# Depthwise convolution of two layers: seven taps off TensorE, eight onto ScalarE with GpSimd, the rest on VectorE

## Chip, cores and metric

The program runs on one core of one Trainium2 chip. The metric is the time of one execution on the device in microseconds; the value before is the median of three runs, 2263.01 us (2261.5 to 2263.6). A profiled execution gives the trace that is read below.

## What is computed

A network of two blocks with two layers each runs over 256 tokens of width 1024 in float32. The change lies in the mixing step of the second block, which occurs twice (once per layer). There, a depthwise convolution of 31 taps runs over 512 channels, and its result goes through a layer norm and a gate into the output product:

```python
CONV_DIM = 512
CONV_WIDTH_2 = 31

c_val, c_gate = jnp.split(c, 2, axis=-1)
c = c_val * jax.nn.sigmoid(c_gate)
c = depthwise_conv(c, conv_w[i], conv_b[i])     # y[s, ch] = b[ch] + sum_j w[j, ch] * c[s + j - 15, ch]
c = jax.nn.silu(layer_norm_2(c, conv_ln_g[i], conv_ln_b[i]))
y_conv = c @ w_conv_out[i]
...
h = h + (g_attn * y_attn + g_conv * y_conv) @ w_o[i]
```

## The kernel before

Activations lie with 128 channels on the partitions and the 256 tokens along the free dimension, so a channel's tap is a column of 128 factors and a shifted window of 256 tokens. Every large product is done in three passes with split operands: `wload` (L133) loads a weight tile of 128x1024 on the SP queue, ScalarE rounds it to `hi` (L145), VectorE takes the remainder as `lo` (L146), and `mm3` (L182) multiplies on TensorE at L184, L185 and L186. In this stage there are six buffers for `hi` and six for `lo` (four in one pool, two in another), so ScalarE can round a tile only when TensorE has finished with the one six tiles earlier.

The mixing step of the second block is `mix_b` (L1118). It multiplies in this order: three pairs of query, key and value columns, then four pairs for the convolution (L1224 to L1228), then eight gate pairs (L1230 to L1235); a pair is 128 output rows twice, two weight tiles and 48 matmuls. After each pair the planner `Order` (L310) is moved on by a fixed cost, and it then emits the small steps of generators that are due: the four steps of attention, two heads each (`attention_b`), and four convolution chunks (`conv`, L1202) of 128 channels each. A number that a generator yields is its own estimate of how long the step lasts. After the last gate pair, `O.finish` (L1267) emits what is left of attention and convolution. Then come the layer norm of the convolution (`norm`, L1240), the product of the attention's result (L1269) beside it, and the product of the convolution's result (L1276). The scheduler of the tile framework sets the final order on each engine's queue; each engine runs its queue in that order.

One chunk of `conv` makes the padded input `cp` (L1208). Its first seven taps (`PTAPS`) are matmuls: ScalarE writes a diagonal matrix `dg` of the tap's factors (L1214) and TensorE multiplies it with a shifted window of `cp` into a PSUM bank `rec` (L1215). ScalarE then moves the sum with the bias to `cy` in SBUF (L1218), and VectorE adds the other 24 taps one by one in place (L1220). The four `cy` are summed on TensorE against a matrix of ones for the mean (L1243), VectorE subtracts it (L1246), and so on through a reciprocal at L1256.

Of the kernel before, what the change touches and what calls it, by code (L numbers as in the profile page):

```python
# [8 lines left out]
F32 = mybir.dt.float32  # L9
F32R = mybir.dt.float32r  # L10
AF = mybir.ActivationFunctionType
# [4 lines left out]
MUL, ADD, SUB, MAX = ALU.mult, ALU.add, ALU.subtract, ALU.max  # L16

S = 256
# [4 lines left out]
C1 = -0.5 * math.exp(-0.5)  # L23
ADA_EVERY = 0.67
ADA_BUFS = 2
PTAPS = 7
ADA_PE = 2
FILL = {("f", 0): ((0, 0), (0, 1)), ("f", 1): ((1, 0), (1, 1))}
PBANKS = (4, 2, 2)
# [1088 lines left out]
def mix_b(G, L, x, l, mp, bias, dbg=None):  # L1118
    nc = G.nc
    mm = nc.tensor.matmul  # L1120
    tt = nc.vector.tensor_tensor
    stt = nc.vector.scalar_tensor_tensor
    act = nc.scalar.activation
    ident = G.c("ident", 128)
# [5 lines left out]
    cwh = L.pool.tile([128, 124], F32, tag="cwh", name=G.nm("cwh"))  # L1130
# [68 lines left out]
    cy = [None] * 4  # L1199
    pmu = []  # L1200

    def conv(i, t):  # L1202
        act(t[:, S:], t[:, S:], AF.Tanh, scale=0.5)
        cp = mp.tile([128, S + 30], F32, tag="cp", name=G.nm("cp"), bufs=3)
        nc.vector.memset(cp[:, 0:15], 0.0)
        nc.vector.memset(cp[:, S + 15:], 0.0)
        yield 0.5
        stt(cp[:, 15:S + 15], t[:, S:], 1.0, t[:, :S], ADD, MUL)  # L1208
        dg = []
        yield 1.0  # L1210
        ps = G.rec()
        for jj in range(PTAPS):
            d = mp.tile([128, 128], F32, tag="dg", name=G.nm("dg"), bufs=4)
            act(d, ident, AF.Copy, scale=cwh[:, jj * 4 + i:jj * 4 + i + 1])  # L1214
            mm(ps[:, :S], d, cp[:, jj:jj + S], start=jj == 0, stop=jj == PTAPS - 1)  # L1215
        yield 0.5 * PTAPS
        y = mp.tile([128, S], F32, tag="cy", name=G.nm("cy"), bufs=4)
        act(y, ps[:, :S], AF.Identity, bias=L.col("cb", i))  # L1218
        for jj in range(PTAPS, 31):
            stt(y, cp[:, jj:jj + S], cwh[:, jj * 4 + i:jj * 4 + i + 1], y, MUL, ADD)  # L1220
            yield 0.6
        cy[i] = y

    for i in range(4):  # L1224
        t = mp.tile([128, 512], F32, tag="cvg", name=G.nm("t"), bufs=1)
        tt(v3(t, 2), v3(pair(3 + i), 2), rb, MUL)
        O.add(f"c{i}", conv(i, t), 0.6)
        O.advance(cost)  # L1228
# [55 lines left out]
    for dp in range(4):  # L1284
        w = G.wload(G.ins["w_o"][l, dp], 2048)
        for i in range(2):
            ps = G.ps()
# [320 lines left out]
```

## Time and profile before

| | before |
|---|---|
| median of 3 runs | 2263.01 us |
| profiled execution, its own time | 2264.67 us |
| span from its first to its last instruction | 2262.9 us |
| TensorE busy | 2204.6 us, 97% |
| VectorE busy | 1681.6 us, 74% |
| ScalarE busy | 1276.6 us, 56% |
| GpSimd busy | 12.7 us |
| mean granted TensorE clock | 0.991 |

The profiled execution lasts 1.8 us longer than its span and 1.7 us longer than the median. A busy TensorE means that some matmul is under way, since their records overlap; it does not mean that matmuls follow each other as fast as they can. Shares over the whole span hide the stage of the change: this stage is about 105 us long in each of two layers (from 1328 us and from 1899 us after the span's start), and it is there that the trace has to be read.

### The profile page before, as it was taken

The numbers are of one execution on the slowest core, as the hardware profiler recorded it, in microseconds if no ns is written. First come the engines' busy times: TensorE is split into PE (matmuls) and PEld (weight loads), VectorE is DVE, ScalarE is ACT, GpSimd is POOL, SyncE is SP. The second block draws the span as 40 slices with busy tenths as digits, with TensorE's granted clock in tenths as the row PEclk, the third lists the DMA queues.
The fourth block names the chain that finished last, engine by engine and source line by source line (L and its number), as shares of the span: only waits on it lengthen the run. The fifth ranks groups of instructions, "written<-read, shape, count | busy, mean of one in ns | idle before, by whom it ended". The sixth has DMA issues, their size and how long they took to land.

```text
span 2262.9 us, 46464 instructions
## 1 busy us (share of the span) xinstructions
PE 2204.6 (97%) x18878; PEld 2134.0 (94%) x18878; DVE 1681.6 (74%) x3041; ACT 1276.6 (56%) x2160; POOL 12.7 (1%) x26
## 2 busy tenths in 40 slices
PE   4999999999999999999999999999999999999999
PEld 4989999999888899999999999999999999999999
DVE  5787878877678878876576569976577656997665
ACT  3575645654567645655454567654465446765444
POOL 0000000000000000000100000000000000000000
PEclk9999999999999999999999999999999999999999
DMA  7644457867554356755775652655566565256553
GB/s 281 195 146 145 139 192 263 271 220 260 187 167 145 121 168 227 264 185 157 177 231 159 199 170 88 203 182 177 164 199 196 165 189 177 94 179 198 182 162 120
DMA packets 127522, 415.35 MB, mean 184 GB/s; under 512 B 15019, under 2 KB 17707, under 8 KB 127308
## 3 DMA queue, kind: packets, MB, share of 16 engines
q1 hardware_dynamic: 124668, 407.23, 57.2%
q0 software_dynamic: 768, 2.10, 0.6%
q8 instruction: 148, 2.42, 0.4%
q10 hardware_dynamic: 1872, 3.06, 0.4%
q14 instruction: 66, 0.54, 0.1%
HBM read 408.92 MB, written 3.41 MB: 182 GB/s over the span
## 4 chain that ended last, share of the span: by engine, by line
PE 61%; DVE 2%; ACT 1%; DMA 1%; issue 0%; SPq 0%; ACTq 0%; DVEq 0%
PE ps L184 19%; PE ps L185 19%; PE ps L186 19%; PE aux L158 1%; PE rec L1215 1%; DMA raw<-in_ffn_in 1%; DVE lo L146 1%; ACT hi L145 0%; PE aux L1104 0%; DMA raw<-in_w_out 0%; PE aux L268 0%; DMA raw<-in_ffn_up 0%; DVE cy L1220 0%; ACT dg L1214 0%; PE aux L282 0%
## 5 line engine op out<-in xcount | busy, mean ns | idle before, releaser
L184 PE MATMUL ps<-h,hi 128*128 128x256 f32 x5088 | 1439.1, 284 | 13.7 <-ACT h L221 8.8
L186 PE MATMUL ps<-h,lo 128*128 128x256 f32 x5088 | 1434.0, 282 | 1.2 <-DVE lo L146 1.2
L185 PE MATMUL ps<-l,hi 128*128 128x256 f32 x4032 | 1136.8, 283 | 4.1 <-DVE l L222 3.9
L145 ACT CAST hi<-raw 128x1024 fp32r<-128x1024 f32 (+1 forms) x724 | 704.4, 976 | 629.2 <-PE ps L185 406.4
L146 DVE TENSOR_TENSOR lo<-raw,hi 128x1024 fp32r<-128x1024 f32 (+1 forms) x724 | 819.5, 1134 | 318.8 <-ACT hi L145 316.5
L184 PEld LDWEIGHTS ps<-h,hi 128*128 128x128 f32 x5088 | 961.5, 189 | 25.2 <-ACT h L221 10.2
L186 PEld LDWEIGHTS ps<-h,lo 128*128 128x128 f32 x5088 | 962.0, 189 | 5.3 <-issue 2.2
L185 PEld LDWEIGHTS ps<-l,hi 128*128 128x128 f32 x4032 | 763.4, 189 | 10.2 <-DVE l L222 4.8
L185 PE MATMUL ps<-h,hi 128*128 128x256 f32 x1056 | 298.9, 283 | 0.0
L185 PEld LDWEIGHTS ps<-h,hi 128*128 128x128 f32 x1056 | 198.6, 188 | 1.9 <-issue 0.5
L221 ACT CAST h<-t 128x256 fp32r<-128x256 f32 x148 | 59.6, 405 | 135.4 <-DVE t L1034 93.6
L222 DVE TENSOR_TENSOR l<-t,h 128x256 fp32r<-128x256 f32 x148 | 62.6, 424 | 50.1 <-ACT h L221 50.0
L362 DVE SCALAR_TENSOR_TENSOR ada<-ada,cact 128x1024 f32<-128x1024 f32 x80 | 96.6, 1215 | 2.1 <-DMA ada<-in_w_ada 2.1
L1031 DVE TENSOR_TENSOR t<-ps,r 128x512 f32<-128x512 f32 x88 | 60.7, 690 | 39.3 <-PE ps L186 39.0
L1220 DVE SCALAR_TENSOR_TENSOR cy<-cp,cwh,cy 128x256 f32<-128x256 f32 x192 | 85.1, 477 | 3.2 <-ACT cy L1218 2.9
L235 ACT ACTIVATE t<-x 128x256 f32<-128x256 f32 x96 | 37.6, 406 | 16.8 <-DVE x L1002 7.7
L1034 DVE TENSOR_TENSOR t<-t,t 128x256 f32<-128x256 f32 x88 | 36.8, 419 | 7.2 <-ACT t L1033 7.2
L1033 ACT ACTIVATE t<-t 128x256 f32<-128x256 f32 x88 | 36.2, 412 | 8.5 <-DVE t L1031 7.6
L210 PE MATMUL ps<-hi,h 128*128 128x256 f32 x128 | 37.7, 294 | 0.0
L242 DVE TENSOR_TENSOR t<-t,t 128x256 f32<-128x256 f32 x87 | 36.5, 419 | 1.6 <-ACT t L237 0.3
L212 PE MATMUL ps<-lo,h 128*128 128x256 f32 x128 | 37.4, 293 | 0.0
L248 PE MATMUL aux<-ones,t 128*128 128x1 f32 x68 | 11.0, 267 | 20.9 <-DVE t L242 17.5
(325 smaller groups left out, 1959.8 us busy)
## 6 DMA issues: line engine op xcount, KB each, us to landing
raw<-in_w_in SPq DMA_DIRECT2D x176, 512.0 KB, 4.4
raw<-in_ffn_in SPq DMA_DIRECT2D x176, 512.0 KB, 4.5
raw<-in_ffn_up SPq DMA_DIRECT2D x88, 512.0 KB, 4.6
ada<-in_w_ada SPq DMA_DIRECT2D x80, 512.0 KB, 5.0
raw<-in_ffn_out SPq DMA_DIRECT2D x64, 384.0 KB, 3.1
raw<-in_ffn_out SPq DMA_DIRECT2D x64, 320.0 KB, 3.1
raw<-in_w_branch SPq DMA_DIRECT2D x24, 512.0 KB, 3.8
raw<-in_ffn_down SPq DMA_DIRECT2D x32, 384.0 KB, 3.5
```

What stands on the lines that cost most here:

```text
L145: nc.scalar.copy(hi[:, :m], raw[:, :m])
L146: nc.vector.tensor_tensor(lo[:, :m], raw[:, :m], hi[:, :m], SUB)
L184: mm(ps, w[0], x[0], start=first, stop=False)
L185: mm(ps, w[0], x[1], start=False, stop=False)
L186: mm(ps, w[1], x[0], start=False, stop=last)
L210: mm(ps[:, :256], x[k][0][:, sl], h, start=k == 0, stop=False)
L221: nc.scalar.copy(h, src)
L222: nc.vector.tensor_tensor(l, src, h, SUB)
L235: nc.scalar.square(sq, x[k])
L362: nc.vector.scalar_tensor_tensor(raw, raw, 1.0, cact, MUL, MUL, accum_out=mods[f // 8][:, f % 8:f % 8 + 1]))
L1031: nc.vector.tensor_tensor(v3(gu, 2), v3(ps, 2), rb, MUL)
L1220: stt(y, cp[:, jj:jj + S], cwh[:, jj * 4 + i:jj * 4 + i + 1], y, MUL, ADD)
```

## The change

The matmul taps and their diagonal matrices are gone, and the accumulators lie in SBUF. Of a chunk's 31 taps, tap 0 goes to ScalarE together with the bias, taps 1 to 22 stay on VectorE, and the last eight (`GTAPS`) are multiplied on ScalarE: the first into a second accumulator `cyg`, each of the other seven into one buffer `cyt`, from which GpSimd adds it to `cyg`. At the end VectorE adds `cyg` to `cy`. Chunks 2 and 3 begin their taps only when chunk 0 and chunk 1 are done.

```diff
-PTAPS = 7
+GTAPS = 8
...
-        dg = []
+        def wt(jj):
+            return cwh[:, jj * 4 + i:jj * 4 + i + 1]
+
+        def other(jj):
+            if jj == 31 - GTAPS:
+                act(yg, cp[:, jj:jj + S], AF.Copy, scale=wt(jj))
+            else:
+                u = mp.tile([128, S], F32, tag="cyt", name=G.nm("cyt"), bufs=1)
+                act(u, cp[:, jj:jj + S], AF.Copy, scale=wt(jj))
+                nc.gpsimd.tensor_tensor(yg, yg, u, ADD)
         yield 1.0
-        ps = G.rec()
-        for jj in range(PTAPS):
-            d = mp.tile([128, 128], F32, tag="dg", name=G.nm("dg"), bufs=4)
-            act(d, ident, AF.Copy, scale=cwh[:, jj * 4 + i:jj * 4 + i + 1])
-            mm(ps[:, :S], d, cp[:, jj:jj + S], start=jj == 0, stop=jj == PTAPS - 1)
-        yield 0.5 * PTAPS
+        while i >= 2 and cy[i - 2] is None:
+            yield 0.5
         y = mp.tile([128, S], F32, tag="cy", name=G.nm("cy"), bufs=4)
-        act(y, ps[:, :S], AF.Identity, bias=L.col("cb", i))
-        for jj in range(PTAPS, 31):
-            stt(y, cp[:, jj:jj + S], cwh[:, jj * 4 + i:jj * 4 + i + 1], y, MUL, ADD)
+        acc, yg = y, mp.tile([128, S], F32, tag="cyg", name=G.nm("cyg"), bufs=2)
+        act(acc, cp[:, 0:S], AF.Identity, scale=wt(0), bias=L.col("cb", i))
+        rest = list(range(31 - GTAPS, 31))
+        for jj in range(1, 31 - GTAPS):
+            if rest and jj % 2:
+                other(rest.pop(0))
+            stt(acc, cp[:, jj:jj + S], wt(jj), acc, MUL, ADD)
             yield 0.6
+        tt(y, acc, yg, ADD)
         cy[i] = y
```

In VectorE's queue, the end of the first layer's convolution stood like this before; the first row is the last of the eight gate pairs, L1220 are taps, L146 are the remainders of weight tiles, L1246 begins the norm:

```order
L1232 TENSOR_TENSOR gate_17837<-ps_17850,r_16494 128x512
L1220 SCALAR_TENSOR_TENSOR cy_17266<-cp_17063,cwh_16496,cy_17266 128x256
L146 TENSOR_TENSOR lo_17973<-raw_17970,hi_17972 128x1024
L1220 SCALAR_TENSOR_TENSOR cy_17266<-cp_17063,cwh_16496,cy_17266 128x256
L146 TENSOR_TENSOR lo_18055<-raw_18052,hi_18054 128x1024
L1220 SCALAR_TENSOR_TENSOR cy_17266<-cp_17063,cwh_16496,cy_17266 128x256
L146 TENSOR_TENSOR lo_18061<-raw_18058,hi_18060 128x1024
L222 TENSOR_TENSOR l_17951<-aux_17934,h_17950 128x256
L1246 SCALAR_TENSOR_TENSOR cy_16968<-rec_18002,cy_16968 128x256
```

The same place of VectorE's queue now (taps are L1229, the addition of the second accumulator is L1231, the norm begins at L1256); between the last gate pair and the first row here stand 15 taps and one L222:

```order
L222 TENSOR_TENSOR l_17931<-aux_17920,h_17930 128x256
L1229 SCALAR_TENSOR_TENSOR cy_17655<-cp_17018,cwh_16496,cy_17655 128x256
L1231 TENSOR_TENSOR cy_17533<-cy_17533,cyg_17534 128x256
L1229 SCALAR_TENSOR_TENSOR cy_17655<-cp_17018,cwh_16496,cy_17655 128x256
L146 TENSOR_TENSOR lo_17967<-raw_17964,hi_17966 128x1024
L1229 SCALAR_TENSOR_TENSOR cy_17655<-cp_17018,cwh_16496,cy_17655 128x256
L146 TENSOR_TENSOR lo_17973<-raw_17970,hi_17972 128x1024
L1229 SCALAR_TENSOR_TENSOR cy_17655<-cp_17018,cwh_16496,cy_17655 128x256
L146 TENSOR_TENSOR lo_18055<-raw_18052,hi_18054 128x1024
L1231 TENSOR_TENSOR cy_17655<-cy_17655,cyg_17656 128x256
L1283 SCALAR_TENSOR_TENSOR gate_17048<-gate_17048,ps_17976 128x512
```

Between the last gate pair and the norm there were three taps; now there are 19 and two additions.

In ScalarE's queue, in the middle of the first layer's convolution, rows stood like this before, with the semaphores that each waits for (L145 rounds a weight tile, L1214 makes diagonal matrices):

```order
L145 CAST hi_17198<-raw_17196 128x1024 [waits DMAHW1_49,PE_49]
L145 CAST hi_17204<-raw_17202 128x1024 [waits DMAHW2_49,PE_49]
L1203 ACTIVATE t_16876<-t_16876 128x256 [waits DVE_49,Activation_49]
L1214 ACTIVATE dg_16955<-ca,cwh_16496 128x128 [waits PE_49]
L1214 ACTIVATE dg_16958<-ca,cwh_16496 128x128 [waits PE_49]
L1214 ACTIVATE dg_16961<-ca,cwh_16496 128x128 [waits PE_49]
```

The same queue now (L1217 is a tap's product for GpSimd, L1224 starts an accumulator):

```order
L1217 ACTIVATE cyt_17033<-cp_16842,cwh_16496 128x256 [waits Pool_49]
L1224 ACTIVATE cy_17533<-cp_16936,vec_5351,cwh_16496 128x256 [waits DVE_49]
L1217 ACTIVATE cyt_17043<-cp_16766,cwh_16496 128x256 [waits Pool_49]
L145 CAST hi_17230<-raw_17228 128x1024 [waits DMAHW3_49,PE_49]
L1217 ACTIVATE cyt_17120<-cp_16842,cwh_16496 128x256 [waits Pool_49]
L1217 ACTIVATE cyt_17129<-cp_16766,cwh_16496 128x256 [waits Pool_49]
L145 CAST hi_17236<-raw_17234 128x1024 [waits DMAHW4_49,PE_49]
```

Products for GpSimd stand between the roundings of weight tiles, and each of them waits for GpSimd's addition of the one before.

## Rows read from the trace of the kernel before

**Rows 1.** The page: engines' busy time, share of the span, instructions.

```profile
PE 2204.6 (97%) x18878; PEld 2134.0 (94%) x18878; DVE 1681.6 (74%) x3041; ACT 1276.6 (56%) x2160; POOL 12.7 (1%) x26
```

**Rows 2.** Windows: stretch, length, busy time by engine, granted clock, DMA share, GB/s.

```profile
1328.03:1419.29 91.26, 91.15 (x692) 83.99 (x691) 84.93 (x200) 66.50 (x137) 0.00 (x0) 1.00 0.34 105
1419.29:1432.20 12.91, 12.87 (x92) 10.62 (x91) 11.68 (x19) 8.49 (x15) 0.00 (x0) 1.00 0.69 210
...
1899.45:1990.40 90.95, 90.83 (x691) 83.69 (x690) 84.84 (x199) 66.31 (x136) 0.00 (x0) 1.00 0.34 106
```

**Rows 3.** Instructions of line L1215: nanoseconds minimum/median/maximum, first and last start.

```profile
L1215 PE MATMUL rec<-cp,dg x112: 377/378/483, 1334.4 to 1967.1; 128*128 128x256 f32 x112
```

**Rows 4.** Chain that ended last, 1250 to 1450 us: start, length, what.

```profile
1352.51 3.02 PE rec L1215 x14
...
1393.05 3.22 PE rec L1215 x14
```

**Rows 5.** Groups on VectorE, 1328.03 to 1432.2 us: count, busy us, mean ns, idle before.

```profile
L1220 DVE SCALAR_TENSOR_TENSOR cy<-cp,cwh,cy 128x256 f32<-128x256 f32 x96 | 42.5, 477 | 1.6 <-ACT cy L1218 1.4
L146 DVE TENSOR_TENSOR lo<-raw,hi 128x1024 fp32r<-128x1024 f32 x24 | 28.9, 1217 | 0.3 <-ACT hi L145 0.3
...
L222 DVE TENSOR_TENSOR l<-aux,h 128x256 fp32r<-128x256 f32 x4 | 1.7, 420 | 0.6 <-ACT h L221 0.6
```

**Rows 6.** Timeline of VectorE, first layer: start, length, line, instruction, count.

```profile
1347.00 4.56 DVE L1220 SCALAR_TENSOR_TENSOR cy<-cp,cwh,cy 128x256 f32<-128x256 f32 x11
...
1419.29 0.69 DVE L1232 TENSOR_TENSOR gate<-ps,r 128x512 f32<-128x512 f32 x1
...
1422.95 0.47 DVE L1220 SCALAR_TENSOR_TENSOR cy<-cp,cwh,cy 128x256 f32<-128x256 f32 x1
...
1432.20 1.75 DVE L1256 RECIPROCAL crs<-crs 128x256 f32<-128x256 f32 x1 [0.43 <-ACT crs L1254]
```

**Rows 7.** Waits of VectorE, 1328.03 to 1419.29 us: total us, times, longest.

```profile
DVE cp L1208 <- ACT t L1203: 1.9, 2, 1.1
DVE cy L1220 <- ACT cy L1218: 1.4, 2, 1.1
DVE hv L1152 <- ACT hv L1150: 1.1, 1, 1.1
```

**Rows 8.** Groups on ScalarE, 1328.03 to 1419.29 us.

```profile
L145 ACT CAST hi<-raw 128x1024 fp32r<-128x1024 f32 x23 | 24.0, 1046 | 19.6 <-PE ps L185 19.6
L1214 ACT ACTIVATE dg<-ca,cwh 128x128 f32<-128x128 f32 x24 | 8.2, 392 | 0.6 <-PE rec L1215 0.4
```

**Rows 9.** Groups on GpSimd, whole span.

```profile
L794 POOL MEMSET wz<- 128x512 f32 x4 | 2.1, 544 | 396.5 <-PE ps L186 343.3 <-PE aux L186 53.2
L379 POOL MEMSET lora<- 128x1024 f32 x2 | 1.9, 955 | 175.4 <-issue 175.1 <-POOLq L1599 0.3
```

**Rows 10.** Timeline of GpSimd, 231 to 233 us.

```profile
231.05 0.96 POOL L379 MEMSET lora<- 128x1024 f32 x1 [175.09 <-issue]
```

**Rows 11.** Timeline of VectorE, 230 to 233.5 us.

```profile
230.67 1.22 DVE L146 TENSOR_TENSOR lo<-raw,hi 128x1024 fp32r<-128x1024 f32 x1
231.81 0.48 DVE L700 SCALAR_TENSOR_TENSOR y<-y,vec,bv 128x256 f32<-128x256 f32 x1
```

**Rows 12.** Windows around 1116 us, between the blocks; columns as in rows 2.

```profile
1116.00:1119.00 3.00, 0.99 (x4) 1.00 (x5) 1.01 (x1) 1.24 (x2) 0.53 (x1) 0.75 1.07 177
1119.00:1122.00 3.00, 3.00 (x20) 2.94 (x18) 0.29 (x2) 0.12 (x1) 0.78 (x2) 0.69 1.12 141
...
1125.00:1130.00 5.00, 5.00 (x34) 5.00 (x34) 4.63 (x10) 0.75 (x2) 0.53 (x1) 0.73 1.05 207
```

**Rows 13.** Waits of TensorE, 1095 to 1130 us: total us, times, longest.

```profile
PE ps L184 <- ACT hi L145: 2.2, 1, 2.2
```

## The prediction, made before the change was run

> **What bounds the kernel now.** I began with the page's busy times [rows 1]: TensorE 97%, VectorE 74%. Over the span that says that a matmul saved is time saved. The windows of the stage say something else [rows 2]. From the end of the first convolution pair to the last gate pair (the front, 91.26 us in the first layer) TensorE is busy for 91.15 us, and VectorE for 84.93 us; in the second layer it is the same within 0.3 us. So two engines are full there, and 6.3 us of VectorE's time are free. Part of that is waiting which no one can use: for the tanh ahead of `cp` 1.9 us, for the accumulator that ScalarE takes from PSUM 1.4 us, for a square root 1.1 us [rows 7]. Then, from the last gate pair to the reciprocal of the norm (the tail, 12.9 us), the last tap starts at 1422.95 us, 3.7 us after the gate row at 1419.29 us [rows 6]. ScalarE has room in the front: 66.5 of 91.3 us busy [rows 2], and it waits 19.6 us there for TensorE to free a buffer for the next rounded tile [rows 8]. GpSimd does nothing in either stretch [rows 2].
>
> **What TensorE loses.** 112 passes are removed, 56 per layer [rows 3]. Their records last 378 ns, but they overlap: in the chain of waits a run of 14 (one chunk) stands with 3.02 and 3.22 us [rows 4]. I take 3.1 us, four runs per layer: **12.4 us per layer** off TensorE, all of them in the front. With nothing else in the way the front would last 91.3 - 12.4 = 78.9 us. That is the most that the change can give: 24.8 us.
>
> **What VectorE loses and gains.** A tap costs 0.41 us in a run of them (11 in 4.56 us [rows 6]). It had 24 taps per chunk, it keeps 22 and gets one plain addition of 128x256, for which the L222 row is the nearest, 0.42 us [rows 5]. Per layer that is 8 taps fewer (-3.3 us) and 4 additions more (+1.7 us): -1.6 us. So VectorE hardly gets lighter, and the 7 taps of TensorE have not gone to it but to ScalarE and GpSimd. What does change is where its taps stand. The order rows show 19 taps behind the last gate pair where there were 3, because chunks 2 and 3 start late, and two additions and one L222 more ahead of the norm. For the front this is 24 taps fewer (69 instead of 93): -9.8 us, +0.8 us for the two additions that lie in it, -0.4 us for the L222 that left it, so 84.9 becomes **75.5 us**. The wait for PSUM goes too, so of the 6.3 us of idle time 4.9 stay. VectorE then needs 80.4 us for the front, more than TensorE's 78.9.
>
> **The tail.** The norm needs all four accumulators, and nothing of the taps behind the last gate pair can start earlier, since VectorE runs its queue in order: 16 taps (6.6 us), two additions (0.8 us) and one L222 (0.4 us) are **+7.8 us per layer**, on a stretch where the norm's chain (mean, subtraction, squares, reciprocal) follows. TensorE has the attention's products and the output product of attention to cover with, but the remainders of those weight tiles stand behind most of these taps in the same queue, so I count the 7.8 us whole. In the tail TensorE will stand idle for a few us at a time. What that does to its clock can be read between the blocks: a wait of 2.2 us [rows 13] is followed by granted clocks of 0.75, 0.69 and 0.73 in windows up to 1130 us [rows 12]. Over the 14 us from 1116 us that is about a quarter lost, 3.4 us if the matmuls there were the bound; below, this is 0 in the sum and 3.4 us per layer in the range.
>
> **What GpSimd and ScalarE gain.** ScalarE loses 28 diagonal matrices of 0.39 us per layer [rows 8] and 4 copies from PSUM, and gets 36 products of 128x256: about even, and it has the room. New is GpSimd's addition, 28 per layer, nearly all of them in the front. The trace shows no GpSimd instruction that reads SBUF. The nearest rows are memsets: 544 ns for 512 elements and 955 ns for 1024 [rows 9], so 0.80 ns per element and 0.13 us fixed; 256 elements written are 0.34 us, and with two operands read at the same price each 0.75 us. What one addition costs the stage lies between **0 and 0.75 us**. For 0 speaks that beside the memset at 231.05 us [rows 10] a remainder and a product on VectorE took 1.22 and 0.48 us [rows 11], as elsewhere [rows 5]; but a memset reads nothing. For the upper end speaks the order: there is one buffer `cyt`, so each product on ScalarE waits for the addition before it, and the rounding of weight tiles stands behind that wait; while ScalarE stands, so after a while does VectorE, which takes the remainder, and TensorE. Below zero is excluded, since the addition takes no work off VectorE that is not counted already. I take **0.4 us**, about the middle: 28 x 0.4 = 11.2 us per layer.
>
> The Trainium skill bears on this at one place. Its page "SBUF — State Buffer", section "Who interferes with whom", says that a VectorE instruction with two inputs in SBUF and a GpSimd instruction that reads SBUF exclude each other, and that whichever comes second stands until the first is done; no run here shows it, and the memset beside VectorE agrees with it only in so far as a memset reads nothing. The page "GPSIMD Engine Reference", section 3.1, gives 4497 ns for an addition of 2048 elements, from which I estimate 0.70 us for 256; by that, 28 x 0.70 = 19.6 us would come to a layer and the sum would end near 2296 us.
>
> **The sum.** Per layer: front, VectorE's 75.5 us of work, 11.2 us for the additions and 4.9 us of waits, 91.6 us against 91.3: +0.3 us. Tail: +7.8 us. Together +8.1 us, for two layers +16.2 us. The profiled execution (2264.7 us; its span is 1.8 us shorter) would become 2280.9 us, and the median, 1.7 us below it, 2263.0 + 16.2 = **2279 us**: slower by 0.7%. What TensorE is relieved of is lost twice, to additions that hold up the engines that feed it, and to a tail that no longer has matmuls beside it.
>
> **The rivals.** First, the additions cost nothing: GpSimd's slots lie between ScalarE's waits for TensorE (19.6 us in the front [rows 8]) and disturb no one. Then the front takes 80.4 us (-10.9), the tail +7.8: -3.1 us per layer, -6.2 in all, **2257 us**. This is the one on the other side; it decides at a price of 3.1 / 28 = 0.11 us per addition, below which the kernel is faster. For it speak the undisturbed instructions beside the memset and ScalarE's spare time, against it the one buffer. Second, each addition holds VectorE or ScalarE up for all of its 0.75 us: 21 us, front 101.4 us (+10.1), +17.9 us per layer, **2299 us**. For it speaks that all but the first product of each chunk waits for GpSimd in ScalarE's queue, against it that ScalarE has 24.8 us to spare in the front [rows 2]. The rule of "SBUF — State Buffer" would lead here, too, since VectorE's taps and remainders, 71 of its 97 us from 1328 us to the reciprocal, take two operands from SBUF [rows 2, 5]. Third, the terms cancel: an addition costs 0.03 to 0.19 us, or the scheduler's late taps cost less than counted since weight tiles are ready ahead; then **2263 us** within 4.5. That the matmuls stay is no rival, the order shows them gone.
>
> **How the numbers follow.** A measurement of this kernel can tell about 0.2%, 4.5 us, from no change. Additions at a middling price, 2268 to 2290 us: 0.40. Full price, above 2290 us: 0.22. Additions free, below 2258.5 us: 0.22. Cancelling: 0.16. So faster 0.22, same 0.16, slower 0.62. The likeliest case has 2279 us. The range leaves out the upper part of the full price with the clock on top (2299 + 6.8 us) and the lower part of the free one (VectorE filled without a gap, 2 x 4.9 us less): 2254 to 2299 us.
>
> **What would show it.** The tail from the last gate row to the reciprocal should grow from 12.9 to about 20.7 us, with TensorE idle in it and perhaps a clock below 1.00. The front should have VectorE busy or standing for all of it, TensorE no longer at 100%. If an addition costs its time, taps (0.48 us) and remainders (1.22 us) beside GpSimd get longer, or ScalarE's waits for GpSimd appear ahead of L145; if both stay away, the first rival holds. A median below 2258 us, or a tail of under 15 us, would make my prediction wrong at the additions or at the tail.

## The result, and the profile after

The changed kernel takes **2286.1 us** in the median of four runs (2283.4 to 2291.5), against 2263.3 us of the kernel before in the same comparison: a ratio of 1.0103, with a 95% interval of 1.0089 to 1.0116. It is slower by 1.0%. The forecast was 2279 us in a range of 2254 to 2299.

The page answers to [rows 1] with this line (columns as there):

```profile
PE 2194.3 (96%) x18766; PEld 2124.0 (93%) x18766; DVE 1695.4 (74%) x3033; ACT 1287.7 (56%) x2168; POOL 62.4 (3%) x82
```

112 matmuls are gone and TensorE is busy for 10 us less, yet the span went from 2262.9 to 2285.1 us. The windows of the stage show where the 22.2 us come from. The columns are those of [rows 2]: length, busy time of TensorE, its weight loads, VectorE, ScalarE and GpSimd, granted clock. For each layer there are four windows here: the front (first convolution pair to last gate pair), the tail (to the reciprocal), the stretch to the first row of the convolution's product, and from there to the last row of output.

```profile
1327.81:1416.10 88.29, 81.78 (x644) 76.18 (x642) 82.32 (x177) 71.87 (x144) 24.31 (x28) 0.98 0.34 109
1416.10:1437.73 21.63, 18.32 (x119) 15.29 (x120) 20.79 (x39) 10.66 (x18) 0.67 (x1) 0.92 0.40 121
1437.73:1450.39 12.66, 7.11 (x46) 6.62 (x45) 10.34 (x21) 7.60 (x16) 0.00 (x0) 0.73 0.63 208
1450.39:1481.83 31.44, 31.44 (x267) 31.27 (x266) 26.61 (x43) 18.20 (x30) 0.00 (x0) 1.00 0.65 202
1907.19:1997.40 90.21, 82.88 (x648) 77.28 (x647) 83.05 (x176) 71.84 (x144) 24.64 (x28) 0.96 0.34 106
1997.40:2022.51 25.11, 22.08 (x117) 18.05 (x116) 20.97 (x40) 10.74 (x17) 0.00 (x0) 0.73 0.34 106
2022.51:2036.21 13.70, 8.15 (x46) 7.65 (x45) 10.20 (x18) 7.60 (x16) 0.00 (x0) 0.75 0.57 190
2036.21:2067.65 31.44, 31.44 (x267) 31.28 (x266) 26.60 (x43) 18.20 (x30) 0.00 (x0) 1.00 0.64 202
```

The last two stretches were not shown for the kernel before; its windows of the first layer read:

```profile
1432.20:1445.00 12.80, 12.65 (x103) 12.08 (x102) 11.42 (x20) 8.99 (x17) 0.00 (x0) 1.00 0.44 142
1445.00:1474.35 29.35, 29.35 (x248) 29.12 (x246) 26.32 (x44) 18.10 (x30) 0.00 (x0) 1.00 0.69 241
```

The front is shorter by only 3.0 and 0.9 us, although TensorE is busy for 9.4 and 8.1 us less in it; it now idles there for 6.5 and 7.3 us, where it was full before. Most of that idle time is one wait in each layer, 4.1 us in the first and 4.8 us in the second, for a row that VectorE reaches late (total us, times, longest; first layer):

```profile
PE aux L290 <- DVE t L1158: 4.1, 1, 4.1
```

The kernel before has no wait of TensorE in its front. The tail grew from 12.9 us in the first layer and 13.0 in the second to 21.6 and 25.1 us. The last stretch grew from 29.4 to 31.4 us, with 267 matmuls in it instead of 248: TensorE used to run ahead beside the norm, with 103 matmuls between the reciprocal and the product, and now it has 46 there: of the other 57, 27 stand in the longer tail (119 instead of 92) and 19 in the last stretch. Summed over both layers, from the anchors of the timelines: front -3.9, tail +20.8, behind it +5.2 us, which is 22.1 of the 22.2 us. (The second layer's last gate row stood at 1990.54 us before, so its front was 91.1 us and its tail 13.0.)

In the first layer's tail VectorE has no gap to speak of: 20.8 of 21.6 us are busy (21.0 of 25.1 in the second). Its timeline (start, length, line, instruction, count) answers to [rows 6]:

```profile
1416.10 0.68 DVE L1242 TENSOR_TENSOR gate<-ps,r 128x512 f32<-128x512 f32 x1
1416.70 4.43 DVE L1229 SCALAR_TENSOR_TENSOR cy<-cp,cwh,cy 128x256 f32<-128x256 f32 x11
...
1428.91 0.42 DVE L1231 TENSOR_TENSOR cy<-cy,cyg 128x256 f32<-128x256 f32 x1
...
1437.73 1.75 DVE L1266 RECIPROCAL crs<-crs 128x256 f32<-128x256 f32 x1
```

The chain of waits (start, length, what) tells why TensorE can't cover this:

```profile
1416.78 4.35 DVE cy L1229 x11
1421.13 0.35 DVE l L222
1421.52 1.30 PE aux L158 x8
1422.85 0.38 ACT h L221
```

The remainder `l` (L222) that attention's last step needs stands in VectorE's queue behind eleven taps, and the accumulators and the remainders of weight tiles stand behind still more. TensorE, which has run out of gate pairs, does what little is ready in between, and its waits in the tail are short: 0.5 us for this `l`, 0.4 us for a remainder, and the longest for the accumulator whose addition (L1231) comes after 16 taps:

```profile
PE rec L1253 <- DVE cy L1231: 1.6, 1, 1.6
```

Behind the tail it stands once more, for the norm's own chain, as its waits between the reciprocal and the product show (total us, times, longest):

```profile
PE ps L184 <- ACT h L221: 5.4, 1, 5.4
```

The kernel before shows no wait of TensorE's matmuls in either stretch.

In the front the taps got longer. These are all taps of the program, then GpSimd's additions (nanoseconds minimum/median/maximum, first and last start), then the groups of VectorE in the first layer's front (count | busy us, mean ns | idle before):

```profile
L1229 DVE SCALAR_TENSOR_TENSOR cy<-cp,cwh,cy x176: 437/476/1045, 1333.0 to 2010.3; 128x256 f32<-128x256 f32 x176
```

```profile
L1218 POOL TENSOR_TENSOR cyg<-cyg,cyt x56: 722/742/1702, 1333.9 to 1996.5; 128x256 f32<-128x256 f32 x56
```

```profile
L1229 DVE SCALAR_TENSOR_TENSOR cy<-cp,cwh,cy 128x256 f32<-128x256 f32 x69 | 37.0, 569 | 0.0
L146 DVE TENSOR_TENSOR lo<-raw,hi 128x1024 fp32r<-128x1024 f32 x17 | 20.8, 1248 | 0.3 <-ACT hi L145 0.3
```

A tap's mean there is 569 ns against 477 [rows 5]. How it comes about is seen where the two timelines are laid side by side. First VectorE, then GpSimd:

```profile
1335.34 1.02 DVE L1229 SCALAR_TENSOR_TENSOR cy<-cp,cwh,cy 128x256 f32<-128x256 f32 x1
...
1391.66 1.28 DVE L1085 SCALAR_TENSOR_TENSOR sc<-aux,bias 128x512 f32<-128x512 f32 x2
1392.86 1.26 DVE L1087 TENSOR_REDUCE st<-sc 128x2 f32<-128x512 f32 x2
...
1394.70 2.89 DVE L146 TENSOR_TENSOR lo<-raw,hi 128x1024 fp32r<-128x1024 f32 x2
```

```profile
1335.34 0.74 POOL L1218 TENSOR_TENSOR cyg<-cyg,cyt 128x256 f32<-128x256 f32 x1 [0.62 <-ACT cyt L1217]
...
1392.08 0.74 POOL L1218 TENSOR_TENSOR cyg<-cyg,cyt 128x256 f32<-128x256 f32 x1 [0.63 <-ACT cyt L1217]
1393.44 0.74 POOL L1218 TENSOR_TENSOR cyg<-cyg,cyt 128x256 f32<-128x256 f32 x1 [0.62 <-ACT cyt L1217]
1394.80 1.70 POOL L1218 TENSOR_TENSOR cyg<-cyg,cyt 128x256 f32<-128x256 f32 x1 [0.62 <-ACT cyt L1217]
```

At 1335.34 us tap and addition start together, and the tap takes 1.02 us instead of 0.48, 0.54 us more; that is less than the addition's whole 0.74 us. At 1394.80 us it is first the other way round: the addition begins 0.1 us after a remainder and takes 1.70 us instead of 0.74. The second remainder of that pair then stands in its turn: the pair takes 2.89 us instead of 2.35 (as it is in the kernel before at 1370.46 us), again 0.54 us more. At 1392.08 and 1393.44 us nothing is stretched: there VectorE runs a row with one operand in PSUM (`aux`) and a reduction with a single operand, which take 1.28 and 1.27 us in the kernel before, too. So it looks as if an addition and a VectorE instruction with two operands in SBUF take turns, whichever comes second waiting inside its own record. The Trainium skill, "SBUF — State Buffer", section "Who interferes with whom", says that two such instructions exclude each other and that the order of issue decides which of them waits; these rows agree with it.

### The profile page after: what moved, and what is told of

Same layout as the page of the kernel before. It is cut to its first block, busy times and chain, and to the rows that moved or that the text cites. A ratio compares the mean times of both kernels' runs of the same rounds, so it can differ in the third digit from the quotient of the medians.

```text
span 2285.1 us, 46286 instructions
## 1 busy us (share of the span) xinstructions
PE 2194.3 (96%) x18766; PEld 2124.0 (93%) x18766; DVE 1695.4 (74%) x3033; ACT 1287.7 (56%) x2168; POOL 62.4 (3%) x82
## 4 chain that ended last, share of the span: by engine, by line
PE 57%; DVE 6%; DMA 1%; ACT 1%; issue 1%; POOL 0%; SPq 0%; DVEq 0%; ACTq 0%
PE ps L185 18%; PE ps L186 18%; PE ps L184 18%; DVE cy L1229 2%; DVE lo L146 1%; DMA raw<-in_ffn_in 1%; PE aux L158 0%; ACT hi L145 0%; DMA raw<-in_ffn_up 0%; DVE gate L1242 0%; POOL cyg L1218 0%; PE aux L268 0%; DMA raw<-in_w_out 0%; PE aux L290 0%; DVE l L222 0%
## 5 line engine op out<-in xcount | busy, mean ns | idle before, releaser
L184 PE MATMUL ps<-h,hi 128*128 128x256 f32 x5088 | 1447.8, 286 | 23.5 <-ACT h L221 19.6
L145 ACT CAST hi<-raw 128x1024 fp32r<-128x1024 f32 (+1 forms) x724 | 704.7, 976 | 633.8 <-PE ps L185 416.9
L146 DVE TENSOR_TENSOR lo<-raw,hi 128x1024 fp32r<-128x1024 f32 (+1 forms) x724 | 820.5, 1137 | 322.2 <-ACT hi L145 319.6
L184 PEld LDWEIGHTS ps<-h,hi 128*128 128x128 f32 x5088 | 968.7, 191 | 37.6 <-ACT h L221 20.7
L222 DVE TENSOR_TENSOR l<-t,h 128x256 fp32r<-128x256 f32 x148 | 62.7, 424 | 48.9 <-ACT h L221 48.9
L1229 DVE SCALAR_TENSOR_TENSOR cy<-cp,cwh,cy 128x256 f32<-128x256 f32 x176 | 90.6, 552 | 0.1
L1218 POOL TENSOR_TENSOR cyg<-cyg,cyt 128x256 f32<-128x256 f32 x56 | 49.6, 886 | 822.9 <-ACT cyt L1217 768.9
```

The costliest lines, as they stand in the source:

```text
L145: nc.scalar.copy(hi[:, :m], raw[:, :m])
L146: nc.vector.tensor_tensor(lo[:, :m], raw[:, :m], hi[:, :m], SUB)
L184: mm(ps, w[0], x[0], start=first, stop=False)
L222: nc.vector.tensor_tensor(l, src, h, SUB)
L1218: nc.gpsimd.tensor_tensor(yg, yg, u, ADD)
L1229: stt(acc, cp[:, jj:jj + S], wt(jj), acc, MUL, ADD)
```

## The experiments

Each kernel was compared with the kernel before, whose median was 2264.55 us beside the first three experiments and the one with chunk 2 early, 2262.28 us beside the other four, and 2263.3 us beside the changed kernel. The table gives the length of the two stretches in both layers, from the same anchor rows of VectorE's timeline as above; they belong to one profiled execution each, the medians to 4 to 12 runs.

| kernel | front, us | tail, us | median, us | ratio to before |
|---|---|---|---|---|
| before | 91.3 / 91.1 | 12.9 / 13.0 | 2263.3 | 1 |
| after | 88.3 / 90.2 | 21.6 / 25.1 | 2286.1 | 1.0103 (1.0089 to 1.0116) |
| no additions | 78.8 / 78.8 | 22.7 / 23.7 | 2265.8 | 1.0007 (0.9994 to 1.0019) |
| GpSimd only writes | 78.7 / 78.7 | 23.5 / 23.8 | 2265.8 | 1.0008 (0.9994 to 1.0021) |
| two buffers `cyt` | 87.9 / 88.0 | 22.2 / 22.4 | 2285.6 | 1.0097 (1.0083 to 1.0112) |
| additions on VectorE | 84.5 / 83.1 | 27.1 / 27.1 | 2285.6 | 1.0103 (1.0086 to 1.0120) |
| before, with idle additions | 101.5 / 104.4 | 12.9 / 12.9 | 2289.3 | 1.0122 (1.0105 to 1.0139) |
| before, chunks 2 and 3 late | 88.1 / 88.1 | 32.5 / 32.5 | 2294.0 | 1.0148 (1.0133 to 1.0163) |
| chunk 2 early | 94.5 / 96.0 | 21.0 / 21.1 | 2284.6 | 1.0087 (1.0072 to 1.0102) |
| chunk 2 early, no additions | 87.0 / 87.3 | 21.3 / 21.3 | 2275.1 | 1.0061 (1.0046 to 1.0076) |

The first question was what the additions cost and by which way: by ScalarE's queue, which waits for the one buffer `cyt`, or by VectorE's operands. The second was what the tail costs on its own.

### Without the additions

```diff
                 act(u, cp[:, jj:jj + S], AF.Copy, scale=wt(jj))
-                nc.gpsimd.tensor_tensor(yg, yg, u, ADD)
```

> The changed kernel without GpSimd's 56 additions; ScalarE makes all products, but seven taps of each chunk are left out of the sum. VectorE's order is the same, with 19 taps behind the last gate pair. Ports and queue together: VectorE's busy time in the front falls from 82.3 us to the counted 75.5, the front by 5 to 7 us per layer: 2286 - 10 to - 14 = 2272 to 2276 us, every tap back at 0.48 us. What is left above 2263 us is the tail: 9 to 13 us. If the tail were all, 2286 us stays.

It comes out level with the kernel before, at 2265.8 us, 6 us below the expected 2272 to 2276: the front falls by 9.5 and 11.4 us instead of 5 to 7. The windows of front and tail, first layer, then the front of the second:

```profile
1329.14:1407.95 78.81, 78.51 (x636) 73.74 (x635) 74.11 (x176) 71.30 (x145) 0.00 (x0) 1.00 0.40 121
1407.95:1430.66 22.71, 19.75 (x129) 16.55 (x128) 20.79 (x38) 10.16 (x17) 0.00 (x0) 0.92 0.40 112
...
1900.96:1979.76 78.80, 78.50 (x636) 73.72 (x635) 74.10 (x176) 71.28 (x145) 0.00 (x0) 1.00 0.39 121
```

Against the kernel before, the front is 12.5 and 12.3 us shorter, and TensorE is full in it again: that is the matmul taps' whole time. Against this kernel the additions cost 88.3 - 78.8 = 9.5 and 90.2 - 78.8 = 11.4 us, or 0.34 and 0.41 us for each of the 28. VectorE's busy time in the front falls by 8.2 us in the first layer (82.32 to 74.11) and by 9.0 in the second (83.05 to 74.10), 0.29 and 0.32 us for each addition; the rest of their price is VectorE's idle time. How the price reaches TensorE is seen at the row that it waited for above. First the changed kernel, then the one without additions:

```profile
1357.43 0.95 DVE L1158 TENSOR_TENSOR t<-hv,hv 128x512 f32<-128x512 f32 x1
```

```profile
1354.65 0.68 DVE L1158 TENSOR_TENSOR t<-hv,hv 128x512 f32<-128x512 f32 x1
```

From the front's first row that is 29.6 us with additions and 25.5 without. VectorE comes 4.1 us late there, which is TensorE's wait of 4.1 us (4.8 and 4.8 us in the second layer); without additions TensorE does not wait for it. And yet nothing is won, since tail and what follows give 12.3 us back in the first layer and 13.7 in the second. So even if the additions had cost nothing, the change would have been no gain.

### GpSimd writes, and reads nothing

The addition is replaced by a memset of 128x512, which no result depends on.

```diff
-                u = mp.tile([128, S], F32, tag="cyt", name=G.nm("cyt"), bufs=1)
-                act(u, cp[:, jj:jj + S], AF.Copy, scale=wt(jj))
-                nc.gpsimd.tensor_tensor(yg, yg, u, ADD)
+                u = mp.tile([128, 2 * S], F32, tag="cyt", name=G.nm("cyt"), bufs=1)
+                act(u[:, :S], cp[:, jj:jj + S], AF.Copy, scale=wt(jj))
+                nc.gpsimd.memset(u, 0.0)
...
-        rs = mp.tile([128, S], F32, tag="crs", name=G.nm("crs"), bufs=1)
+        rs = G.tmp(S)
```

> The changed kernel with a memset of 512 elements into the product's buffer (0.54 us) in place of each addition: GpSimd is as often at work and ScalarE waits for it as before, but GpSimd reads nothing; seven taps of each chunk are left out of the sum. If an addition holds VectorE up because it reads SBUF (ports), taps are 0.48 us again and the time falls as in the run without additions, to 2272 to 2277 us. If any instruction on GpSimd holds VectorE up, or ScalarE's waits are the cost (queue), it stays within 4 us of 2286, less the 0.2 us by which a memset is shorter, 28 times per layer at most.

All GpSimd work of this kind, and the taps beside it:

```profile
L1218 POOL MEMSET cyt<- 128x512 f32 x56 | 29.5, 527 | 821.9 <-ACT cyt L1217 821.9
```

```profile
L1229 DVE SCALAR_TENSOR_TENSOR cy<-cp,cwh,cy x176: 431/476/485, 1330.9 to 1988.8; 128x256 f32<-128x256 f32 x176
```

Each GpSimd instruction lasts 527 ns, ScalarE's products wait for some of them, and still the front is 78.7 us and no tap exceeds 485 ns; the median of 2265.8 us is again below the expected range. With additions the longest took 1045 ns. A memset of this length costs nothing; what costs is that the addition reads. ScalarE's waits are fewer here, though (us, times; 13.3 and 17 with the additions), so what they cost is left to the next run:

```profile
  ACT cyt L1217: 4.9, 8
```

(An addition is 0.2 us longer, 742 ns; that this alone should turn 0 into 10 us per layer does not fit the stretched taps.)

### Two buffers for the products

```diff
-                u = mp.tile([128, S], F32, tag="cyt", name=G.nm("cyt"), bufs=1)
+                u = mp.tile([128, S], F32, tag="cyt", name=G.nm("cyt"), bufs=2)
...
-        rs = mp.tile([128, S], F32, tag="crs", name=G.nm("crs"), bufs=1)
+        rs = G.tmp(S)
```

> The changed kernel with two buffers for the products that GpSimd adds, so that ScalarE need not wait for each addition (the norm's reciprocal lies in a shared buffer to make room). If ScalarE's waits for GpSimd cost the time (theory: queue; 6.7 us of them in the first layer's front), 2286 - 13 = 2273 us and these waits gone. If the additions hold up VectorE whenever they run (ports), or the late taps make it (tail), 2286 +- 3 us with taps as long as in the changed kernel.

With one buffer, all of ScalarE's waits for GpSimd come to this (us, times), and with two to the second row:

```profile
  ACT cyt L1217: 13.3, 17
```

```profile
  ACT cyt L1217: 3.6, 12
```

Three quarters of the wait are gone, and the time is the same: 2285.6 against 2286.1 us. The queue of ScalarE, which the prediction named first for the upper end, is not the price. (The trace of this kernel is of one of its shorter executions, 2282.6 us: its first layer is as in the changed kernel, its second is 2.2 us shorter in front and 2.7 in the tail, with a clock of 0.92 there against 0.73.)

### The additions on VectorE

```diff
-                nc.gpsimd.tensor_tensor(yg, yg, u, ADD)
+                nc.vector.tensor_tensor(yg, yg, u, ADD)
```

> The changed kernel with the 56 additions on VectorE in place of GpSimd. On GpSimd they cost the stage 9.5 us in the first layer's front (88.3 against 78.8 us without them), 0.34 us each; on VectorE an addition of 128x256 takes 0.34 us from start to start where several follow each other, 28 x 0.34 = 9.5 us per layer. If GpSimd's additions take VectorE's time while they run (ports), nothing is gained by having them on GpSimd: 2286 +- 5 us. If the additions cost the time in another way (the way over a second engine and its waits), VectorE alone is faster: 2275 us or less. VectorE's order has 26 taps behind the last gate pair in place of 19, which may add up to 2.9 us per layer.

The time is again that of the changed kernel, 2285.6 us, with another split: a front 4 to 7 us shorter, and a tail 2 to 5.5 us longer, where 26 taps and eight of the additions stand now. (The profiled execution is the longest of its four, 2293.1 us, but what it is longer by lies ahead of the stage: the first layer's front begins at 1335.5 us instead of 1327.8.) Handing the addition to GpSimd gained nothing over doing it on VectorE itself: the price there, 0.34 to 0.41 us, is also what a VectorE addition takes (0.42 us by its record here, 0.34 us from its start to that of the next row).

### The kernel before, with additions that nobody needs

Here GpSimd adds seven windows of `cp` per chunk into a scratch tile beside the VectorE taps; all of the original work is done as it was.

```diff
+    yg = mp.tile([128, S], F32, tag="cyg", name=G.nm("cyg"), bufs=1)
+    nc.gpsimd.memset(yg, 0.0)
...
         for jj in range(PTAPS, 31):
+            if jj < 2 * PTAPS:
+                nc.gpsimd.tensor_tensor(yg, yg, cp[:, jj:jj + S], ADD)
             stt(y, cp[:, jj:jj + S], cwh[:, jj * 4 + i:jj * 4 + i + 1], y, MUL, ADD)
...
-        rs = mp.tile([128, S], F32, tag="crs", name=G.nm("crs"), bufs=1)
+        rs = G.tmp(S)
```

> The kernel before with 56 more additions on GpSimd, seven per chunk, which add a window of the padded input to a scratch tile that no one uses; no engine waits for them but for the padded input's buffer. If they hold VectorE up (ports; 8.2 us more busy time per front in the changed kernel), VectorE's 84.9 us in the front become 93, more than the front's 91.3: +2 to +9 us per layer, 2267 to 2281 us, with taps of up to 1 us. If only their place in the chain of the convolution cost time, 2263 +- 4 us.

Fronts of both layers, and the taps up to the reciprocal of the first:

```profile
1326.72:1428.24 101.52, 93.13 (x692) 85.53 (x691) 94.53 (x200) 66.38 (x137) 24.70 (x28) 0.98 0.31 94
1908.00:2012.35 104.35, 97.53 (x692) 88.78 (x691) 94.51 (x200) 66.62 (x137) 24.69 (x28) 0.93 0.30 92
```

```profile
L1224 DVE SCALAR_TENSOR_TENSOR cy<-cp,cwh,cy 128x256 f32<-128x256 f32 x96 | 49.3, 547 | 1.3 <-ACT cy L1220 1.1
```

TensorE's work and VectorE's instructions are the same in number as in [rows 2], but VectorE is busy for 94.5 us instead of 84.9, 0.34 us for each of 28 additions, and the front is longer by 10.3 and 13.3 us, 0.37 and 0.47 us for each addition. A tap's mean is 547 ns against 477 [rows 5]; the tail, in which GpSimd adds nothing, stays at 12.9 us. This is the price of the additions with no other part of the change around it, and it is no smaller than in the changed kernel. No engine waits for GpSimd here. The median of 2289.3 us is above the expected 2267 to 2281: VectorE's 6.3 us of idle time in the front [rows 2] did not take up any of it (101.5 - 94.5 = 7.0 us are still idle).

### The kernel before, chunks 2 and 3 late

```diff
         yield 1.0
+        while i >= 2 and cy[i - 2] is None:
+            yield 0.5
         ps = G.rec()
```

> The kernel before with one line more: chunks 2 and 3 start only when chunks 0 and 1 are done. Nothing is on GpSimd, the matmul taps stay. VectorE's order then has 43 taps behind the last gate pair in place of 3. If late taps make a tail that nothing covers (tail): 40 x 0.41 = 16.4 us more tail per layer, less what TensorE can still do in it, two chunks' matmuls of 3.1 us each: about +10 us per layer, 2284 us. If TensorE's freed time were lost otherwise, and the place of the taps does not matter, 2263 +- 4 us.

The late start was carried over without anything else. 43 taps now stand behind the last gate pair, the front is 3.2 us shorter, the tail 19.6 us longer, the stretch from reciprocal to product 2.1 us shorter, and the last one 31.5 us long, 2.2 more: +16.4 us for the first layer's stage, and 2294.0 us in all, 10 more than expected. The 40 taps more are 40 x 0.41 = 16.4 us by the price of [rows 6], and VectorE's busy time in the tail grew by 16.7 us (28.4 against 11.7). In the front VectorE is busy for 10.5 us less (74.4 us), but this brings the front nothing, since TensorE fills it, 88.0 of 88.1 us; its 3.2 us are the 14 matmul taps that left with them (678 matmuls instead of 692). So taps that move behind the last gate pair out of a front that TensorE fills cost their whole time there. That the stage's total is the same 16.4 us is in part chance, since the front's 3.2 us are set off by VectorE's idle time in the tail, 4.1 us instead of 1.2.

### Chunk 2 early

Chunk 2 no longer waits for chunk 0; chunk 3 still does.

```diff
-        while i >= 2 and cy[i - 2] is None:
+        while i >= 3 and cy[0] is None:
             yield 0.5
...
-        acc, yg = y, mp.tile([128, S], F32, tag="cyg", name=G.nm("cyg"), bufs=2)
+        acc, yg = y, mp.tile([128, S], F32, tag="cyg", name=G.nm("cyg"), bufs=3)
...
-        rs = mp.tile([128, S], F32, tag="crs", name=G.nm("crs"), bufs=1)
+        rs = G.tmp(S)
```

> The changed kernel, but chunk 2 starts its taps at once and only chunk 3 waits, for chunk 0 (three accumulators on GpSimd's side; the norm's reciprocal lies in a shared buffer to make room). In VectorE's queue 10 taps then stand behind the last gate pair in place of 19. If the late taps make the tail (theory: tail), 9 x 0.41 = 3.7 us per layer go from the tail, more if the slow clock goes with them: 2286 - 7 to - 14 = 2272 to 2279 us. If the loss is the additions on GpSimd holding VectorE up (theory: ports), their number is the same and the time stays at 2286 +- 3 us.

Ten taps are late instead of 19. The tail is 21.0 us all the same, and the front grew to 94.5 and 96.0 us, so that the time is that of the changed kernel within a tenth of a per cent. Nine taps less are 3.7 us by the price of [rows 6], but the tail's window shows VectorE busy for 18.85 us, 1.9 less than in the changed kernel, and idle for 2.2 instead of 0.8. The granted clock is 1.00 there:

```profile
1416.57:1437.59 21.02, 18.96 (x138) 16.20 (x136) 18.85 (x33) 11.36 (x19) 0.00 (x0) 1.00 0.70 220
```

So the count of late taps alone does not set the tail's length; what else is put there, and what it then waits for, counts as well. Nor is a slow clock needed for a tail of 21 us.

### Chunk 2 early, no additions

The same edit, without the line of the addition.

```diff
-                nc.gpsimd.tensor_tensor(yg, yg, u, ADD)
...
-        while i >= 2 and cy[i - 2] is None:
+        while i >= 3 and cy[0] is None:
```

> The run without additions, but chunk 2 starts at once and only chunk 3 waits, for chunk 0: 10 taps behind the last gate pair in place of 19, and VectorE has room in the front (74 of 79 us busy). Seven taps of each chunk are left out of the sum. If the late taps make the tail (tail), 9 x 0.41 = 3.7 us per layer go, and some slow clock with them: 2266 - 7 to - 14 = 2252 to 2259 us. If the norm's chain alone sets the tail, whatever the taps, 2266 +- 4 us.

This missed on the other side: 2275.1 us, slower than with chunk 2 late. The front is 8 us longer than in the kernel that only lacks the additions. Between two gate rows there are 15.5 us (1376.84 to 1392.36 us) where the other kernel has 6.0 (1377.03 to 1383.00), with 73 matmuls instead of 53. That window, TensorE's waits in it, and its timeline:

```profile
1376.84:1392.36 15.52, 12.71 (x73) 10.57 (x72) 13.10 (x37) 11.42 (x29) 0.00 (x0) 0.78 0.28 88
```

```profile
PE aux L1104 <- ACT sc L1098: 2.8, 1, 2.8
```

```profile
1381.09 1.89 PE L1104 MATMUL aux<-ca,sc 128*128 128x128 f32 x8 [2.81 <-ACT sc L1098]
```

With the taps in another order, an attention step comes to stand where TensorE has to wait 2.8 us for ScalarE's products (L1098), and the matmuls of the next 4 us follow each other at 0.21 us instead of 0.12. So the order around the early taps costs more than they bring; that the early taps themselves cost nothing is not shown. The kernel above, with chunk 2 early and the additions, has a wait for the same row, 3.3 us in the first layer. Set against each other, these two kernels give another price of the additions: 7.6 and 8.7 us in the fronts and 9.5 us in the median, where it was 20.3 us with chunk 2 late. So the price hangs on the order, too. Whether an order exists that has both, the short front and a short tail, none of these runs shows.

## Why the prediction was right, and where it was off

The sign, the size and the case are those that were forecast: +22.8 us in the median against +16.2, in the case of additions at a middling price (2268 to 2290 us). Point by point:

**TensorE's 12.4 us** are right to a tenth: without the additions the front lasts 78.8 us, and 78.9 was the floor.

**VectorE's part in the front** was put at 75.5 us of work and 4.9 of waits, 80.4 us. Without the additions it is 74.1 us of work, and the front ends with TensorE's 78.8: a term 1.6 us too high. With them VectorE sets the pace, as the sum had it: it is 4.1 us late at the row that TensorE waits for.

**The additions' 0.4 us each** hold: 0.34 in one layer and 0.41 in the other, against bounds of 0 and 0.75. The value was right, the way to it only half: it was a middle between two bounds, so that it came so near is luck. The order's one buffer was given as what speaks for the upper end, and it does nothing that can be measured (two buffers: a quarter of the waits, same time). What costs is the operands, which the prediction had beside its sum and in one of its rivals. Of the 0.72 to 0.75 us that an undisturbed addition lasts, less than half reaches VectorE's busy time (0.29 and 0.32 us): in the rows above an addition costs VectorE 0.54 us where it strikes, and some fall on instructions that do not mind them, as at 1392.08 us. The full-price rival falls for that reason. The rival of free additions falls in two ways: they are not free, and with them gone the kernel is at 2265.8 us, not at the 2257 that it promised.

**The tail's 7.8 us** were too small, and this is the step that was mis-sized. It measured +8.7 and +12.1 us, and without additions +9.8 and +10.7. The taps themselves are as counted. What the sum left out stands around them. First, VectorE's busy time in the tail rose by 9.1 us, from 11.7 to 20.8, and not by 7.8: besides the taps and additions there are one remainder and two gate rows (L1283) more in it, while the L222 that the sum added was there before. In the first layer this is the whole of it, since VectorE is idle for only 0.8 us there, so the clock of 0.92 can have cost little. In the second VectorE's busy time is nearly the same (21.0 us), but it stands for 4.1 us, for products of TensorE and for a rounding on ScalarE that had itself waited for TensorE:

```profile
DVE gate L1283 <- PE ps L186: 2.3, 3, 1.8
DVE l L222 <- ACT h L221: 1.8, 1, 1.8
```

The granted clock in that tail is 0.73, and it is 3.5 us longer than the first. So the clock, which was 0 in the sum and up to 3.4 us per layer in the range, is the likely cause there; no run changed the clock by itself. Second, TensorE's idle time in the tail and behind it comes back as matmuls that are still to be done: the last stretch has some 20 more, +2.1 and +2.4 us. The prediction ended its sum at the reciprocal, as if nothing behind it could change. Over both layers the profiled executions have -3.9 us in the front (forecast +0.6), +20.8 in the tail (+15.6) and +5.2 behind it (0). The front's gain on the forecast and the tail's loss nearly cancel, which is luck, and the stretch that was not counted is about what the forecast was short of: 22.1 against 16.2 us.

**What should be seen** was seen: a tail near 20.7 us (21.6 and 25.1), TensorE idle in it (3.3 and 3.0 us), a clock below 1.00, longer taps (mean 569 ns), and ScalarE's waits for GpSimd (6.7 us in the first front). Of the last two, only the first was a price. That VectorE would be busy or standing for the whole front is true of any front; TensorE no longer being at 100% was the telling part, 81.8 of 88.3 us.

What stays open is why the granted clock differs in the two tails. Ahead of the last gate row both layers look the same; behind it the rows part:

```profile
1410.00:1416.10 6.10, 4.36 (x38) 4.15 (x36) 5.73 (x16) 6.06 (x17) 1.83 (x3) 1.00 0.01 3
1416.10:1420.00 3.90, 3.51 (x22) 2.33 (x22) 3.90 (x11) 3.21 (x6) 0.67 (x1) 1.00 0.00 0
```

```profile
1991.00:1997.40 6.40, 4.45 (x39) 4.25 (x38) 6.29 (x15) 5.83 (x16) 2.17 (x3) 1.00 0.00 0
1997.40:2001.00 3.60, 3.05 (x14) 1.36 (x12) 3.60 (x10) 2.89 (x4) 0.00 (x0) 0.59 0.01 2
```

One keeps the level of 2.4 GHz, the other falls to nearly 1.2, after TensorE had stood for 1.81 and 1.95 us just ahead of the gate rows. The first layer falls to that level later and for a shorter time (0.50 from 1426 to 1428 us, 1.00 again from 1428), after the wait of 1.6 us for the accumulator. No run was made that sets this idle time, and with two buffers both tails have 0.92.

## What to carry to other kernels

An addition of two SBUF operands is no cheaper on GpSimd than on VectorE when VectorE runs two-operand instructions beside it: here it cost the front 0.34 to 0.41 us, and the program took the same time with the additions on either engine. Taking matmuls off a full TensorE pays only if the work behind the last matmul of the stage gets no longer; here, even without the additions, some 12.4 us won in the front were paid back in full by 16 taps that moved behind it and by TensorE's idle time there, which came back further on. Sum such a change past the stretch it touches, up to the next point where all engines are in step again.

## What the runs showed of the hardware that was not expected

The collision reaches very small instructions. The product of two columns at L1154 (128x8) takes 0.16 us in the kernel before and 0.68 us here, where an addition of GpSimd had begun 0.06 us earlier; first VectorE, then GpSimd:

```profile
1354.35 0.68 DVE L1154 TENSOR_TENSOR hv<-hv,hv 128x8 f32<-128x8 f32 x1
```

```profile
1354.29 0.72 POOL L1218 TENSOR_TENSOR cyg<-cyg,cyt 128x256 f32<-128x256 f32 x1 [0.62 <-ACT cyt L1217]
```

The wait stands inside the record, so it counts as busy time: set against the kernel without additions, VectorE's 82.3 us in the front are 74.1 us of work and 8.2 us of standing, and no view of waits has them. GpSimd's own records stretch in the same way, from 0.74 to 1.70 us. Where the addition comes first, the wait has nearly the same length whatever the row: 0.52 us for the product above, 0.54 us for the tap and the remainder in the front.
